# Stick-breaking attention stage: ScalarE in written order, VectorE's written order begun later, q's second copies read from SBUF, and three more products ahead of the last scores

## The chip, the cores and the metric

The kernel runs on one core of one Trainium2 chip. The metric is the device time of one execution in microseconds (us). Of the kernel before, three executions were timed and one more was run under the hardware profiler. "PE" is TensorE (matmuls; "PEld" its weight loads), "ACT" is ScalarE, "DVE" is VectorE, "POOL" is GpSimd, "SP" is the queue that issues the loads.

## The reference, cut to what matters

Two layers over 512 tokens of width 1024, in float32: layer 0 mixes tokens by stick-breaking attention (16 heads of 64), layer 1 by a gated MLP, and each is followed by a SwiGLU feed-forward part. The change lies in layer 0's attention:

```python
qkv = (h @ w_qkv).reshape(B, S, 3, SB_HEADS, SB_HEAD_DIM)
z = einsum('bhtd,bhsd->bhts', q_block, k[:, :, :kend]) * SB_HEAD_DIM ** -0.5
log_1m = where(before, log_sigmoid(-z), 0.0)
later = cumsum(log_1m, reverse=True) - log_1m
a = where(before, exp(log_sigmoid(z) + later), 0.0)
o = einsum('bhts,bhsd->bhtd', a, v[:, :, :kend])
y = o.transpose(0, 2, 1, 3).reshape(B, S, D) @ w_o
```

With s = sigmoid(-z), a weight is the difference of two neighbours in the running product of s. The kernel takes it so: tokens are laid out in reverse, a scan multiplies the sigmoids up, and a subtraction of the scan from itself, shifted by one, gives the weights.

## The kernel before, in words

**Precision.** A float32 product is done as three fast products (`mm3`): each operand is split into a high part rounded to fp32r and a low part, the rest. `split` makes the high part on ACT (L112, tiles named `wh` for weights) and the low part on DVE (`wl`).

**Weights.** All weight blocks of 512 KB stand in one list, `stream`, in the order of use. `wload` issues the next block's load on SP into one of two buffers (`raw`). `wemit` splits the next block into one of five buffer pairs (`wh`, `wl`). `wget(src, look=3)` is called where a block is used and first runs `wemit` up to three blocks further. While `dve.chain` is set, `wemit` also issues the load of the block after, ahead of the split. The condition vector's sums (`Bg`, tiles `G`, `A`, `B`, loads `rawada` in two buffers of their own) are advanced one step at a time by `bg.step`, one multiply-add on DVE per step.

**Order of work.** The framework puts each engine's instructions in an order by a plan of its own, which can move an instruction far ahead of its place in the program. Two chains overrule it: where `pe["chain"]` is set, matmuls go in written order, and the class `Written` does the same for an engine while its `chain` is set. Before the change only DVE is wrapped (`dve = Written(nc.vector)`); ACT (`act = nc.scalar`) follows the framework's plan throughout. Both chains are set at L861, just before the first pair's `evac_q`, and cleared at L912.

**The attention stage**, about 61 to 262 us of the profile, has three parts.

1. *The v phase* (L863 to L878). The products of pair 0's q and k and of the first half of v have just ended. `v_evac(0)` copies v out of four PSUM banks, `evac_q` and `evac_k` copy and split q and k, and the second half of v is computed in eight steps of 12 matmuls. Pair 0's first scores stand after step 1, its second scores after step 4.
2. *The lead-in* (L879 to L886). `fill(n)` runs n of the small products that make q and k of the later pairs (`pqk`, three matmuls each; eight make a q or a k; two PSUM banks in turn). 6 fills, pair 0's last scores, then 4, 4 and 6 fills.
3. *The pairs* (L887 to L908), eight turns. A turn transposes the weights of its pair in three groups (`flip`: LATE of 3 blocks a head, EARLY0 of 3, EARLY1 of 4; each copied from PSUM by ACT into `ar`, L834, out of one bank per head, `tw`), computes the next pair's scores in three groups (`scores`: `z` on PE, sigmoid on ACT at L807, scan into `left` and subtraction into `ga` on DVE), multiplies with v (`values`, tile `av`) and splits the result (`finish`, tile `o`). Between them stand fills, seven numbers a turn in `FILLS`, and `Bg` steps in `SUMS`. When q's and k's products have run out, in turns 6 and 7, the fills are the first 16 products of the output projection (tile `y`).

**q's evacuation** (`evac_q`, L693). Each of two heads has its own tile half with the other head's 64 partitions filled too: ACT copies the head's half out of PSUM, scaled by 0.125 (L696); DVE makes the low part `qlow` from PSUM and that copy (L698); ACT copies the same PSUM half, scaled again, into the other 64 partitions (L703). `evac_k` (L706) makes one copy on ACT (L709) and the low part on DVE.

In a turn with fills of 2, 3, 2, 3, 2, 3, 1, the fourth fill ends a q and the twelfth ends a k; the fifth and the thirteenth begin the next product and so call `wget`, which emits one split.

Of the kernel before, what the change touches and what calls it, by code (L numbers as in the profile page):

```python
# [8 lines left out]
F32 = mybir.dt.float32  # L9
F32R = mybir.dt.float32r  # L10
AF = mybir.ActivationFunctionType
# [14 lines left out]
def trunk(ctx: ExitStack, tc: tile.TileContext, A: dict, out: bass.AP):  # L26
    nc = tc.nc
# [19 lines left out]
    def slot(dt, name, a=2, b=512):  # L47
        return s4.tile([P, a, b], dt, tag="s4", name=nm(name))

    def bank(name, tag="b"):  # L50
        return psum.tile([P, 512], F32, tag=tag, bufs=6 if tag == "b" else 2, name=nm(name))

    act = nc.scalar
    pe = {"prev": None, "chain": False}

    class Written:
# [13 lines left out]

            return call

    dve = Written(nc.vector)

    def pe_op(b):

# [607 lines left out]
    with tc.tile_pool(name="att", bufs=1) as att, tc.tile_pool(name="att2", bufs=6) as att2:  # L684
# [3 lines left out]
        own = [slice(0, 64), slice(64, P)]  # L688
# [4 lines left out]
        def evac_q(i, pq):  # L693
            q = slot(F32R, "q")
            for h in range(2):
                act.activation(q[own[h], h, :], pq[own[h], :], AF.Copy, scale=0.125)  # L696
            for h in range(2):
                dve.scalar_tensor_tensor(  # L698
                    qlow[own[h], i % 2, h, :], pq[own[h], :], 0.125,
                    q[own[h], h, :].bitcast(F32), ALU.mult, ALU.subtract,  # L700
                )
            for h in range(2):
                act.activation(q[own[1 - h], h, :], pq[own[h], :], AF.Copy, scale=0.125)  # L703
            qk[i] = [q]

        def evac_k(i, pk):  # L706
# [12 lines left out]
        def filler():  # L719

            for i in range(1, NPAIR):
                for e, evac in enumerate((evac_q, evac_k)):
                    pb = bank("pqk", "p")
                    w = wget(("wqk", i, e))
                    for k in range(KD):
                        h, l = hTk(hT, k, 0, T)
                        mm3(pb[:], w[0][:, k, :], w[1][:, k, :], h, l, k == 0, k == KD - 1)
                        if k == KD - 1:
                            evac(i, pb)
                        yield  # L730
            early["w"].extend(wget(("wo", k), 0) for k in range(NEARLY))
            for tt, y in early["y"].items():
                tok = slice(tt * P, (tt + 1) * P)
                for k, w in enumerate(early["w"]):
                    for hf in range(2):
                        if k == 0:
                            y[hf] = bank("y", "p" if tt == 3 else "b")
                        c = slice(hf * 512, (hf + 1) * 512)
                        mm3(
                            y[hf][:], o8[k][:, 0, tok], o8[k][:, 1, tok],  # L740
                            w[0][:, 0, c], w[1][:, 0, c], k == 0, False,
                        )
                        yield
# [1 line left out]
        NEARLY = 4  # L745
        FIRST = (4, 4, 6)
        FILLS = ((2, 3, 2, 3, 2, 3, 1),) * 5 + (
            (2, 2, 2, 2, 2, 2, 0), (1, 2, 1, 2, 1, 1, 0), (3, 0, 2, 0, 2, 1, 0),
        )
        SUMS = ((0, 1, 0, 1, 0, 0, 0),) * 6 + ((1, 1, 1, 1, 1, 1, 0), (1, 0, 1, 0, 1, 1, 0))  # L750
        fgen = filler()
# [1 line left out]
        def fill(n, at=None):  # L753
            for j in range(n):
                next(fgen, None)
                if j == at:
                    bg.step(1)
# [100 lines left out]

        with tc.issue_after(last_sqrt[0].ins):
            table = nc.scalar.preload_act_table_set("sigmoid_and_others")  # L860
        pe["chain"] = dve.chain = True  # L861
        evac_q(0, pq0)
        evac_k(0, pk0)  # L863
        B31, B2, B0 = (3, 1), (2,), (0,)
# [15 lines left out]
        av = bank("av")  # L880
        spare = bank("spare")
        bg.bank = lambda: spare
        fill(6, 1)
        cur[0](B0)
        for n in FIRST:
# [23 lines left out]
        for _ in fgen:  # L909
            bg.step(1)  # L910
        bg.step(99)
        pe["chain"] = dve.chain = False  # L912

    wpool2 = ctx.enter_context(tc.tile_pool(name="wpool2", bufs=1))
    wpools.append((wpool2, 1))
# [356 lines left out]
```

## Time and profile before

| | us |
|---|---|
| median of 3 executions | 1166.7 (1164.49 to 1168.05) |
| profiled execution | 1164.59 |
| its span, first to last instruction | 1162.8 |
| PE busy | 1119.7 (96%) |
| DVE busy | 869.5 (75%) |
| ACT busy | 567.8 (49%) |

A row of the timeline gives an instruction's start and duration in us, engine, source line, operation, output<-inputs and shape; "x2" after it means that two instructions that follow each other were merged; in square brackets stands how long the engine was idle before and what released it. A row of the waits gives who waited for whom, the total in us, the number of times and the longest. A row of the windows gives, for a stretch of time, its length, the busy time of PE, PEld, DVE, ACT and POOL (with instruction counts), the granted PE clock as a share of full speed, the share of time in which the 16 DMA engines were busy, and GB/s. DVE instructions all carry line L65 (the wrapper's call), matmuls L89, transposes L97. In a pipelined row of matmuls the time from start to start is the pace; the duration of one is longer.

### The profile page before, as it was taken

The numbers are of one execution on the slowest core, as the hardware profiler recorded it, in microseconds if no ns is written. First come the engines' busy times: TensorE is split into PE (matmuls) and PEld (weight loads), VectorE is DVE, ScalarE is ACT, GpSimd is POOL, SyncE is SP. The second block draws the span as 40 slices with busy tenths as digits, with TensorE's granted clock in tenths as the row PEclk, the third lists the DMA queues.
The fourth block names the chain that finished last, engine by engine and source line by source line (L and its number), as shares of the span: only waits on it lengthen the run. The fifth ranks groups of instructions, "written<-read, shape, count | busy, mean of one in ns | idle before, by whom it ended". The sixth has DMA issues, their size and how long they took to land.

```text
span 1162.8 us, 17861 instructions
## 1 busy us (share of the span) xinstructions
PE 1119.7 (96%) x7136; PEld 991.6 (85%) x7136; DVE 869.5 (75%) x1131; ACT 567.8 (49%) x951; POOL 22.0 (2%) x37
## 2 busy tenths in 40 slices
PE   4989999899999999999999999999999999999997
PEld 3767777678999999998877887988999999998886
DVE  6858898967988888778676865668989898882214
ACT  6434665655655555563143633536555555581112
POOL 0200000000000000000000100001000000000000
PEclk8989999999999999999999999999999999999999
DMA  8637343524424353438887474324334444244311
GB/s 325 223 115 243 114 128 92 162 91 145 145 91 150 125 163 128 128 114 281 282 264 235 146 253 128 127 57 163 107 126 117 158 128 145 73 144 146 94 52 73
DMA packets 48775, 173.91 MB, mean 150 GB/s; under 512 B 5674, under 2 KB 6058, under 8 KB 48692
## 3 DMA queue, kind: packets, MB, share of 16 engines
q1 hardware_dynamic: 46964, 166.48, 44.5%
q0 software_dynamic: 1728, 6.29, 1.4%
q8 instruction: 56, 0.92, 0.3%
q14 instruction: 27, 0.22, 0.1%
HBM read 164.36 MB, written 8.39 MB: 149 GB/s over the span
## 4 chain that ended last, share of the span: by engine, by line
PE 68%; DVE 13%; DMA 12%; issue 4%; ACT 3%; SPq 0%; DVEq 0%; ACTq 0%
PE r L89 30%; PE y L89 20%; DMA rawada<-in_ada 6%; PE v L89 4%; PE gu L89 4%; DVE wl L65 3%; PE pqk L89 2%; DMA rawx<-in_wx 2%; PE u L89 2%; DVE left L65 2%; DVE B L65 1%; DMA raw<-in_wqk 1%; DMA raw<-in_wdown 1%; PE tw L97 1%; PE sv L89 1%
## 5 line engine op out<-in xcount | busy, mean ns | idle before, releaser
L89 PE MATMUL y<-wh,as 128*128 128x512 f32 x832 | 263.9, 395 | 0.6 <-DVE G L65 0.6
L112 ACT ACTIVATE wh<-raw 128x1024 fp32r<-128x1024 f32 x112 | 118.3, 1060 | 213.7 <-PE y L89 100.9
L65 DVE TENSOR_TENSOR wl<-raw,wh 128x1024 fp32r<-128x1024 f32 x112 | 136.3, 1221 | 108.5 <-ACT wh L112 108.0
L89 PEld LDWEIGHTS y<-wh,as 128*128 128x128 f32 x832 | 156.2, 188 | 37.5 <-DVE G L65 1.1
L89 PE MATMUL r<-Sh,wl 128*128 128x256 f32 x608 | 170.4, 280 | 0.0
L89 PE MATMUL r<-Sh,wh 128*128 128x256 f32 x608 | 170.1, 280 | 0.0
L89 PE MATMUL r<-Sl,wh 128*128 128x256 f32 x608 | 170.1, 280 | 0.0
L89 PE MATMUL y<-wl,as 128*128 128x512 f32 x416 | 164.3, 395 | 0.0
L65 DVE TENSOR_TENSOR wl<-f,wh 128x1024 fp32r<-128x1024 f32 x76 | 92.7, 1220 | 36.8 <-ACT wh L112 36.8
L112 ACT ACTIVATE wh<-f 128x1024 fp32r<-128x1024 f32 x76 | 80.7, 1062 | 76.0 <-PE r L89 66.2
L89 PEld LDWEIGHTS r<-Sh,wh 128*128 128x128 f32 x608 | 114.7, 189 | 0.0
L89 PEld LDWEIGHTS r<-Sl,wh 128*128 128x128 f32 x608 | 114.6, 188 | 0.0
L89 PEld LDWEIGHTS r<-Sh,wl 128*128 128x128 f32 x608 | 114.6, 188 | 0.0
L89 PEld LDWEIGHTS y<-wl,as 128*128 128x128 f32 x416 | 78.2, 188 | 17.9
L89 PE MATMUL r<-hTh,wh 128*128 128x256 f32 x304 | 88.8, 293 | 1.2 <-DVE gu L65 1.2
L89 PE MATMUL r<-hTl,wh 128*128 128x256 f32 x304 | 84.8, 279 | 0.0
L89 PE MATMUL r<-hTh,wl 128*128 128x256 f32 x304 | 80.1, 280 | 0.0
L89 PEld LDWEIGHTS r<-hTh,wh 128*128 128x128 f32 x304 | 57.2, 188 | 6.5 <-DVE gu L65 2.6
L89 PE MATMUL r<-hTh,b 128*128 128x256 f32 x304 | 60.7, 282 | 0.0
L89 PE MATMUL v<-wh,hTh 128*128 128x512 f32 x128 | 52.9, 413 | 5.1 <-ACT hTh L628 5.1
L89 PE MATMUL v<-wl,hTh 128*128 128x512 f32 x128 | 52.6, 411 | 5.0 <-DVE wl L65 5.0
L89 PEld LDWEIGHTS r<-hTl,wh 128*128 128x128 f32 x304 | 57.3, 188 | 0.1
(197 smaller groups left out, 2444.0 us busy)
## 6 DMA issues: line engine op xcount, KB each, us to landing
rawada<-in_ada SPq DMA_DIRECT2D x80, 512.0 KB, 4.9
raw<-in_wdown SPq DMA_DIRECT2D x44, 512.0 KB, 4.1
rawy<-in_wy SPq DMA_DIRECT2D x38, 512.0 KB, 3.6
rawx<-in_wx SPq DMA_DIRECT2D x38, 512.0 KB, 4.5
raw<-in_wqk SPq DMA_DIRECT2D x16, 512.0 KB, 4.3
ada<-in_ada0p SPq DMA_DIRECT2D x12, 512.0 KB, 8.1
raw<-in_wgu SPq DMA_DIRECT2D x12, 512.0 KB, 4.2
xd<-x POOLq DMA_DIRECT2D x12, 512.0 KB, 2.9
```

The source lines that it names most:

```text
L65: b = f(*a, **k)
L89: b = nc.tensor.matmul(o, l, r, start=start, stop=stop, skip_group_check=True)
L97: last_tp[0] = nc.tensor.transpose(o, i, ident)
L112: act.activation(hi, src, AF.Copy)
```

## The change

```diff
@@ -50,7 +50,6 @@
-    act = nc.scalar
     pe = {"prev": None, "chain": False}
@@ -70,7 +69,7 @@
-    dve = Written(nc.vector)
+    dve, act = Written(nc.vector), Written(nc.scalar)
@@ -700,7 +699,7 @@ (evac_q)
             for h in range(2):
-                act.activation(q[own[1 - h], h, :], pq[own[h], :], AF.Copy, scale=0.125)
+                act.activation(q[own[1 - h], h, :], q[own[h], h, :].bitcast(F32), AF.Copy)
             qk[i] = [q]
@@ -745,7 +744,7 @@
         FILLS = ((2, 3, 2, 3, 2, 3, 1),) * 5 + (
-            (2, 2, 2, 2, 2, 2, 0), (1, 2, 1, 2, 1, 1, 0), (3, 0, 2, 0, 2, 1, 0),
+            (2, 2, 2, 2, 2, 2, 0), (4, 2, 1, 1, 0, 0, 0), (3, 0, 2, 0, 2, 1, 0),
         )
@@ -858,7 +857,7 @@ (ahead of the v phase)
-        pe["chain"] = dve.chain = True
+        pe["chain"] = True
         evac_q(0, pq0)
@@ -880,6 +879,7 @@ (after the v phase)
         bg.bank = lambda: spare
+        dve.chain = act.chain = True
         fill(6, 1)
@@ -909,7 +909,7 @@ (after the last turn)
-        pe["chain"] = dve.chain = False
+        pe["chain"] = dve.chain = act.chain = False
```

It has four edits. ACT is wrapped as DVE is, and from the lead-in to the end of the attention stage it issues in written order. DVE's written order begins at the lead-in, so that in the v phase DVE follows the framework's plan, and `wemit`, which looks at `dve.chain`, issues no load ahead there. q's second copies read the first copy in SBUF in place of PSUM. In turn 6 the eight fills are spread as 4, 2, 1, 1, 0, 0, 0, so that four and no longer one stand ahead of the last pair's first scores.

## The prediction, made before the run

> **What bounds the kernel now.** I read the page first: PE is busy 96% of the span, so time is won only where PE stands still or runs at a low clock. Then I asked for PE's waits from 60 to 270 us, the stage that the change touches.
>
> ```profile
> PE v L89 <- DVE wl L65: 5.0, 1, 5.0
> PE tw L97 <- ACT ar L834: 4.1, 5, 1.8
> PE pqk L89 <- ACT q L703: 2.8, 1, 2.8
> PE z L89 <- DVE k L65: 2.1, 1, 2.1
> ```
>
> Four places, 14.0 us in all. The windows show what else happens at them, and how full the engines are in a turn of the pair loop.
>
> ```profile
> 64.00:70.00 6.00, 1.01 (x3) 0.82 (x3) 4.96 (x6) 3.27 (x6) 0.00 (x0) 0.83 0.00 0
> 70.00:75.00 5.00, 5.00 (x13) 3.83 (x13) 1.39 (x2) 1.68 (x2) 0.00 (x0) 0.52 0.69 213
> 95.30:113.30 18.00, 15.21 (x66) 11.95 (x65) 14.46 (x14) 9.59 (x16) 0.00 (x0) 1.00 0.66 211
> 131.10:150.27 19.17, 18.62 (x110) 14.75 (x109) 17.47 (x21) 11.70 (x22) 0.00 (x0) 1.00 0.31 90
> 226.20:244.10 17.90, 15.77 (x90) 12.26 (x88) 17.67 (x23) 9.87 (x17) 0.00 (x0) 0.90 0.47 148
> ```
>
> Two things are to be seen. In a normal turn (131.10 to 150.27) PE is the fullest engine, 18.62 of 19.17 us, with DVE close behind at 17.47 and ACT far below. And the granted clock is 0.52 right after the 5.0 us wait, and 0.90 around the 2.1 us wait; both stalls cost more than their idle time. So each of the four stalls is walked through, and for each I ask what is late next.
>
> **Part 1: VectorE's order in the v phase.** DVE and ACT around the 5.0 us wait:
>
> ```profile
> 56.58 1.05 ACT L112 ACTIVATE wh<-raw 128x1024 fp32r<-128x1024 f32 x1
> ```
> ```profile
> 64.95 1.39 DVE L65 SCALAR_TENSOR_TENSOR qlow<-pq,q 64x512 fp32r<-64x512 f32 x2 [7.55 <-ACT q L696]
> 66.38 1.39 DVE L65 TENSOR_TENSOR k<-pk,k 64x512 fp32r<-64x512 f32 x2
> 67.80 2.36 DVE L65 TENSOR_TENSOR wl<-raw,wh 128x1024 fp32r<-128x1024 f32 x2
> ```
>
> PE's second half of v waits for the first `wl` at 67.80. Its inputs were there at 56.58 + 1.05 = 57.6, and DVE stood idle for 7.55 us; only the written order, which puts q's and k's low parts first, held it. Without that order nothing holds the two `wl` back, and PE can go on at about 64. Gain 5.0. The slow clock goes with the wait: in the chain of waits 23 matmuls at half clock take 8.21 us, and 9 at full clock took 2.10, 0.233 each.
>
> ```profile
> 50.38 2.10 PE v L89 x9
> 69.08 8.21 PE v L89 x23
> ```
>
> 23 at 0.233 are 5.4, so another 2.8 us are saved. The moved order also takes the extra load ahead out of `wemit` in this phase and lets the sums `G` run early: their loads wait on SP behind the weights'. Neither is on PE's path as long as `qlow` and `k` come by PE's first scores, 24 matmuls or 5.6 us after 64; two such pairs of instructions, 2.78 us from 64.95, end at 67.8, 1.8 us early, and one sum in front of them fits. On the other side, DVE may take up a `wl` just before something of the start that PE needs: at most 2.36 / 2 = 1.2, at best nothing; I take 0.3, since the 7.55 us of idle time are the nearer row.
>
> The Trainium skill (TensorE: Matmul & The Clock Gate, section "Why this matters for your kernels") asks for no PE gap over about 3 us, since one idle window of about 3.4 us halves the clock. The 5.0 us wait and its 0.52 agree with it.
>
> **Part 2: the lead-in.** The third product group needs a PSUM bank that q of pair 1 still holds:
>
> ```profile
> 107.41 0.40 PE L89 MATMUL pqk<-hTh,wl 128*128 128x512 f32 x1
> 110.59 0.50 PE L89 MATMUL pqk<-hTh,wh 128*128 128x512 f32 x1 [2.79 <-ACT q L703]
> ```
> ```profile
> 107.92 1.39 DVE L65 SCALAR_TENSOR_TENSOR qlow<-pqk,q 64x512 fp32r<-64x512 f32 x2
> ```
> ```profile
> 109.35 1.19 ACT L703 ACTIVATE q<-pqk 64x512 fp32r<-64x512 f32 x2 [1.48 <-DVE qlow L65]
> ```
>
> The bank is read by ACT, then DVE, then ACT again. With the copies from SBUF the last reader is `qlow`, so 110.54 - 109.31 = 1.2 us go for certain. The rest hangs on `qlow`, which was late because DVE in the window 95.30 to 113.30 was idle for 3.5 of 18 us, partly behind sums whose loads had not landed:
>
> ```profile
> DVE G L65 <- DMA rawada<-in_ada: 4.5, 4, 1.4
> ```
>
> PE will come here 5.0 + 2.8 = 7.8 us earlier, at about 99.8, so `qlow` must end 109.31 - 99.8 = 9.5 us earlier than it did. DVE gets 2.36 us of `wl` and some sums out of the way before 64, and loses the 4.5 us of load waits if the sums start that early; with the 3.61 us that it idled from 70 to 75 (5.00 less 1.39) that makes 10.5. It just suffices. Bounds: gain 1.2 less nothing to 2.8; I take 2.8, and leave the other end to a rival. The copies themselves: 0.60 us each from PSUM; the nearest ACT row from SBUF, 0.63 for 512 elements on twice the partitions, makes it 0.03 more, hidden on an engine with 7 us of free time a turn.
>
> ```profile
> 236.18 0.63 ACT L112 ACTIVATE acch<-G 128x512 fp32r<-128x512 f32 x1 [0.51 <-PE spare L89]
> ```
>
> **Part 3: ScalarE in written order in the turns.** One turn, SP, ACT, PE, DVE:
>
> ```profile
> 136.30 8.74 SPq L106 DMA_DIRECT2D raw<-in_wqk  x2
> ```
> ```profile
> 139.82 1.06 ACT L112 ACTIVATE wh<-raw 128x1024 fp32r<-128x1024 f32 x1 [3.92 <-DMA raw<-in_wqk]
> 140.78 1.18 ACT L696 ACTIVATE q<-pqk 64x512 fp32r<-64x512 f32 x2
> 141.98 0.87 ACT L834 ACTIVATE ar<-tw 128x384 f32<-128x384 f32 x2
> 143.42 1.20 ACT L703 ACTIVATE q<-pqk 64x512 fp32r<-64x512 f32 x2 [0.28 <-DVE qlow L65]
> ```
> ```profile
> 136.26 0.39 PE L89 MATMUL pqk<-hTh,wl 128*128 128x512 f32 x1
> 137.19 0.82 PE L97 MATMUL tw<-identt,ga 128*128 128x128 f32 x6
> 141.58 0.40 PE L89 MATMUL pqk<-hTh,wl 128*128 128x512 f32 x1
> 142.53 1.09 PE L97 MATMUL tw<-identt,ga 128*128 128x128 f32 x8 [0.55 <-ACT ar L834]
> ```
> ```profile
> 153.93 1.22 DVE L65 TENSOR_TENSOR wl<-raw,wh 128x1024 fp32r<-128x1024 f32 x1
> ```
>
> ACT's planned order puts the `wh` of the next block first. It waits 3.92 us for a load that was issued at 136.30, and it is needed only by the `wl` at 153.93. Behind it stand q, whose products ended at 136.65, and `ar`, which frees the banks for the 8 transposes. In written order q comes first: from 136.65 two q (1.18), two copies (1.20), the `wh` of a block older, whose `wl` is the next (1.06), and two `ar` (0.87) end at 140.96. PE wants the banks at 141.58 + 0.24 = 141.82, so the wait goes with 0.86 us to spare. All five waits of this kind are 4.1. In turn 5 one product fewer (3 x 0.233 = 0.70) lies between, which leaves 0.16; I give back 0.2.
>
> The change queues things behind waits on ACT too: behind q's wait for PE now stand the copies, a split and `ar`; behind the k copies the sigmoids of the last scores. The sum above holds them. DVE gets q about 4 us earlier (140.78 less 136.65); PE, at 18.62 us a turn, is what remains.
>
> **Part 4: four products ahead of the last scores.** PE and DVE in turns 6 and 7:
>
> ```profile
> 227.41 0.40 PE L89 MATMUL y<-wh,o 128*128 128x512 f32 x1
> 229.94 0.33 PE L89 MATMUL z<-k,q 128*128 128x128 f32 x1 [2.13 <-DVE k L65]
> 247.40 0.82 PE L97 MATMUL tw<-identt,ga 128*128 128x128 f32 x6
> ```
> ```profile
> 229.20 1.41 DVE L65 TENSOR_TENSOR k<-pqk,k 64x512 fp32r<-64x512 f32 x2
> 244.26 1.23 DVE L65 TENSOR_TENSOR ga<-left 128x1024 f32<-128x1024 f32 x1
> ```
> ```profile
> 230.00:234.00 4.00, 4.00 (x16) 3.14 (x17) 3.97 (x6) 1.19 (x2) 0.00 (x0) 0.73 0.61 193
> 234.00:238.00 4.00, 4.00 (x21) 3.52 (x20) 4.00 (x6) 2.17 (x5) 0.00 (x0) 0.85 0.33 116
> ```
>
> Three more products take 2.1 us and cover the wait of 2.1. The slow clock after it is worth 4.00 x 0.27 + 4.00 x 0.15 = 1.7. But those products are taken from between these scores and the transposes at 247.40, which need the `ga` that ends at 245.49. DVE works from `k` to that `ga` without a pause (17.67 of 17.90 busy), 245.49 - 229.94 = 15.55 after the scores; PE's way there shrinks from 17.46 to 17.46 - 2.1 - 1.7 = 13.7. So PE waits there for up to 1.9 us, less what DVE is ahead; I take 1.5 back.
>
> By the same rule of the Trainium skill a wait of 2.1 us is too short to halve the clock; the 0.73 behind it disagrees.
>
> **The sum.** 5.0 + 2.8 - 0.3 + 2.8 + 4.1 - 0.2 + 2.1 + 1.7 - 1.5 = 16.5 us. Behind the stage PE hardly waits and takes the gain on. The profiled execution, 1164.59 (span 1162.8 and 1.8 around it), becomes 1148.1; it lies 2.1 below the median of 1166.7, so for the median I say **1150.2**.
>
> **The rivals.**
> - *Half of the front is given back (1155.5).* The framework's plan puts sums that wait for loads ahead of `qlow` and `k` in the v phase: one load wait of up to 1.4 and one sum of 1.3 at the first scores (2.7), and the lead-in keeps 1.6 to 2.8 of its wait. For it: the 10.5 against 9.5 of part 2. Against: PE's 1.8 us of room. 1150.2 + 2.7 + 2.6 = 1155.5.
> - *The clock dip in turn 6 has another cause (1151.9).* Then 1.7 stays. For it: after the 2.79 us wait of the lead-in the clock was 1.00. By the Trainium skill's rule above this would be the case. Against: it is the only dip in the turns, and it lies right behind the wait.
> - *No change (1166.7).* DVE becomes the bound and PE waits for it wherever it gains. For it: 17.47 busy. Against: 18.62 for PE is more, and DVE itself waits for q.
> - *Slower (1173.7).* In written order ACT meets each turn's `wh` before its load has landed, at the place behind the q copies, and waits the 3.92 of above there, with `ar` behind it: six turns x 3.92 = 23.5, so 1150.2 + 23.5. It decides once a load lands later than 139.1 (136.65 + 1.18 + 1.20) for the block whose `wl` is the next one. Against: loads land about one block earlier than that, since the one landed at 139.82 was for a `wl` at 153.93.
>
> **How the numbers follow.** Forecast 0.60, half of the front 0.20, clock 0.08, no change 0.07, slower 0.05. The range 1146 to 1157.5: downward, if nothing is given back (2.0) and pace is won beyond the idle rows, upward to the first rival and its bounds; outside lie the last two and a little of the others. About 0.3%, 3.5 us, is what a measurement of this kernel tells from no change: faster 0.88, same 0.07, slower 0.05.
>
> **What would show it.** Right: PE's wait for `wl` gone, no half clock at 69; the v phase 7.5 us shorter; no wait for ACT q L703; turns of about 18.5 us, each `wh` directly ahead of its `wl` in time and without a wait for a load; a small wait of the transposes on DVE's `ga` in turn 7. Wrong: new PE waits on `qlow` or `k` of pair 0 or 1, ACT idle on loads ahead of `ar`, or turns still of 19.1 us.

## The result, and the profile after

| | before | after |
|---|---|---|
| median (us) | 1166.96 of 4 (1164.49 to 1168.05) | 1151.72 of 4 (1148.75 to 1153.22) |
| profiled execution, its span | 1164.59, 1162.8 | 1153.22, 1151.4 |

The ratio is 0.9869 [0.9844, 0.9894]: faster by 15.2 us, where 16.5 were forecast. The two profiled executions are only 11.4 us apart in span: that of before took 2.4 less than its median, that of after 1.5 more than its own, and 11.4 + 2.4 + 1.5 = 15.3. Before the steps of the prediction are judged, the 11.4 us are laid out by stage.

PE's waits from 60 to 270 us come first, in after. The columns are who waited for whom, the total in us, the times and the longest.

```profile
PE pqk L88 <- DVE qlow L64: 2.1, 1, 2.1
PE y L88 <- DVE k L64: 2.1, 1, 2.1
```

Of 14.0 us in four places, 4.2 are left in two, and both are new. (After has one code line less: matmuls are L88, and DVE and ACT both carry L64, the line of the wrapper.) The marks between the stages are the two evacuations of v on ACT and the products with v (`av`) of pairs 0, 5 and 7 on PE. In before:

```profile
61.79 2.07 ACT L599 ACTIVATE V<-v 128x512 f32<-128x512 f32 x4 [4.16 <-PE v L89]
95.80 2.04 ACT L599 ACTIVATE V<-v 128x512 f32<-128x512 f32 x4
```
```profile
128.78 2.38 PE L89 MATMUL av<-ar,V 128*64 128x128 f32 x24
223.91 2.38 PE L89 MATMUL av<-ar,V 128*64 128x128 f32 x24
252.97 2.38 PE L89 MATMUL av<-ar,V 128*64 128x128 f32 x24
```

In after:

```profile
64.25 2.07 ACT L64 ACTIVATE V<-v 128x512 f32<-128x512 f32 x4 [3.57 <-PE v L88]
89.64 2.06 ACT L64 ACTIVATE V<-v 128x512 f32<-128x512 f32 x4 [3.96 <-PE v L88]
```
```profile
124.26 2.38 PE L88 MATMUL av<-ar,V 128*64 128x128 f32 x24
214.18 2.38 PE L88 MATMUL av<-ar,V 128*64 128x128 f32 x24
242.95 2.38 PE L88 MATMUL av<-ar,V 128*64 128x128 f32 x24
```

Differences of neighbouring marks give the table (us).

| stage | before | after | gain | forecast |
|---|---|---|---|---|
| start to first evacuation of v | 61.79 | 64.25 | -2.46 | -0.3 |
| v phase, to the second | 34.01 | 25.39 | 8.62 | 7.8 |
| lead-in, to `av` of pair 0 | 32.98 | 34.62 | -1.64 | 2.8 |
| five turns, to `av` of pair 5 | 95.13 | 89.92 | 5.21 | 3.9 |
| two turns, to `av` of pair 7 | 29.06 | 28.77 | 0.29 | 2.3 |
| the rest | 909.83 | 908.45 | 1.38 | 0 |
| span | 1162.8 | 1151.4 | 11.4 | 16.5 |

The v phase and the turns did more than was forecast, the lead-in and the last turns failed, and the start lost. How good the turns became is seen in the windows of the first and the fifth of them in after (columns as in the prediction: length, busy time of PE, PEld, DVE, ACT and POOL, granted clock, DMA share, GB/s):

```profile
124.26:142.67 18.41, 18.41 (x109) 14.84 (x109) 17.35 (x21) 11.77 (x22) 0.00 (x0) 1.00 0.37 116
197.85:214.18 16.33, 16.33 (x101) 13.15 (x100) 15.22 (x19) 9.87 (x19) 0.00 (x0) 1.00 0.35 102
```

PE is busy for the whole of each turn: 18.41 of 18.41. Nothing is left to win there by another order. ACT in the first of these turns:

```profile
132.18 1.22 ACT L64 ACTIVATE q<-pqk 64x512 fp32r<-64x512 f32 x2 [0.80 <-PE pqk L88]
133.30 1.27 ACT L64 ACTIVATE q<-q 64x512 fp32r<-64x512 f32 x2
134.59 1.06 ACT L64 ACTIVATE wh<-raw 128x1024 fp32r<-128x1024 f32 x1
135.68 0.87 ACT L64 ACTIVATE ar<-tw 128x384 f32<-128x384 f32 x2
```

q, its copies, a split and `ar` follow each other without a pause, and the split waits for no load, where it had waited 3.92 us. From 124 to 243 us ACT waits for no load at all.

The two new waits as the timeline of PE has them, in the lead-in and in turn 6, and DVE in the v phase, the lead-in and turn 6:

```profile
104.56 0.47 PE L88 MATMUL pqk<-hTh,wh 128*128 128x512 f32 x1 [2.14 <-DVE qlow L64]
...
220.15 0.47 PE L88 MATMUL y<-wh,o 128*128 128x512 f32 x1 [2.08 <-DVE k L64]
```
```profile
73.51 1.28 DVE L64 SCALAR_TENSOR_TENSOR G<-rawada,sc,G 128x1024 f32<-128x1024 f32 x1
...
89.56 1.28 DVE L64 SCALAR_TENSOR_TENSOR G<-rawada,sc,G 128x1024 f32<-128x1024 f32 x1 [1.20 <-DMA rawada<-in_ada]
93.17 1.28 DVE L64 SCALAR_TENSOR_TENSOR G<-rawada,sc,G 128x1024 f32<-128x1024 f32 x1 [2.32 <-DMA rawada<-in_ada]
95.47 1.28 DVE L64 SCALAR_TENSOR_TENSOR G<-rawada,sc,G 128x1024 f32<-128x1024 f32 x1 [1.01 <-DMA rawada<-in_ada]
...
103.03 1.39 DVE L64 SCALAR_TENSOR_TENSOR qlow<-pqk,q 64x512 fp32r<-64x512 f32 x2
...
218.61 1.39 DVE L64 TENSOR_TENSOR k<-pqk,k 64x512 fp32r<-64x512 f32 x2
```

The first sum of the stage runs at 73.51, in the v phase and not ahead of it. DVE then stands idle for 1.20 + 2.32 + 1.01 = 4.5 us in front of sums whose loads have not landed, and `qlow` of pair 1 starts at 103.03, 4.9 us earlier than before (107.92). PE comes for its bank at 104.56 - 2.14 = 102.4, 5.4 earlier than before (110.59 - 2.79). In turn 6 the second of the four products that now stand ahead of the last scores takes the other PSUM bank, and there k of pair 7 lies until DVE has read it at 220.0.

Each of these waits is followed by a stretch at half clock, and the start has one too:

```profile
42.00:62.00 20.00, 18.35 (x81) 14.66 (x80) 14.03 (x25) 8.91 (x12) 5.98 (x8) 0.91 0.43 136
100.00:112.00 12.00, 9.86 (x42) 7.75 (x41) 11.75 (x12) 3.64 (x7) 0.00 (x0) 0.86 0.67 223
216.00:228.00 12.00, 9.92 (x48) 8.05 (x45) 10.56 (x14) 5.83 (x10) 0.00 (x0) 0.86 0.72 218
```

A clock of 0.86 over 12 us is 0.14 x 12 = 1.7 us of PE work lost; 0.09 x 20 is 1.8 (1.7 by windows of 1 us, which show half clock from 47.5 to 51). Before has 1.00 in the first two of these windows; the half clock of its turn 6 lies at 231 to 235 us.

### The profile page after: what moved, and what is told of

Its sections match the earlier page's. It is cut to its first block, busy times and chain, and to the rows that moved or that the text cites. A ratio compares the mean times of both kernels' runs of the same rounds, so it can differ in the third digit from the quotient of the medians.

```text
span 1151.4 us, 17842 instructions
## 1 busy us (share of the span) xinstructions
PE 1118.6 (97%) x7136; PEld 993.1 (86%) x7136; DVE 869.3 (75%) x1131; ACT 568.5 (49%) x951; POOL 22.1 (2%) x37
## 4 chain that ended last, share of the span: by engine, by line
PE 76%; DVE 9%; DMA 9%; issue 3%; ACT 2%; SPq 0%; DVEq 0%; ACTq 0%
PE r L88 32%; PE y L88 20%; PE pqk L88 6%; DMA rawada<-in_ada 5%; PE gu L88 4%; PE v L88 4%; PE u L88 2%; DVE wl L64 2%; PE z L88 2%; PE tw L96 1%; PE av L88 1%; DVE G L64 1%; DMA raw<-in_wdown 1%; PE tp L96 1%; PE sv L88 1%
## 5 line engine op out<-in xcount | busy, mean ns | idle before, releaser
L88 PE MATMUL y<-wh,as 128*128 128x512 f32 x832 | 264.0, 395 | 0.5 <-DVE G L64 0.5
L64 DVE TENSOR_TENSOR wl<-raw,wh 128x1024 fp32r<-128x1024 f32 x112 | 136.3, 1222 | 107.0 <-ACT wh L64 106.7
L64 ACT ACTIVATE wh<-raw 128x1024 fp32r<-128x1024 f32 x112 | 118.2, 1060 | 179.2 <-PE y L88 99.0
L88 PEld LDWEIGHTS y<-wh,as 128*128 128x128 f32 x832 | 156.2, 188 | 37.6 <-DVE G L64 1.0
L88 PE MATMUL r<-Sh,wl 128*128 128x256 f32 x608 | 170.4, 280 | 0.0
L88 PE MATMUL r<-Sh,wh 128*128 128x256 f32 x608 | 170.1, 280 | 0.0
L88 PE MATMUL r<-Sl,wh 128*128 128x256 f32 x608 | 170.1, 280 | 0.0
L88 PE MATMUL y<-wl,as 128*128 128x512 f32 x416 | 164.3, 395 | 0.0
L64 DVE TENSOR_TENSOR wl<-f,wh 128x1024 fp32r<-128x1024 f32 x76 | 92.8, 1222 | 36.7 <-ACT wh L64 36.7
L64 ACT ACTIVATE wh<-f 128x1024 fp32r<-128x1024 f32 x76 | 80.7, 1061 | 74.7 <-PE r L88 64.9
L88 PEld LDWEIGHTS r<-Sh,wh 128*128 128x128 f32 x608 | 114.7, 189 | 0.0
L88 PEld LDWEIGHTS r<-Sl,wh 128*128 128x128 f32 x608 | 114.6, 188 | 0.0
L88 PEld LDWEIGHTS r<-Sh,wl 128*128 128x128 f32 x608 | 114.6, 188 | 0.0
L88 PEld LDWEIGHTS y<-wl,as 128*128 128x128 f32 x416 | 78.2, 188 | 17.9
L88 PE MATMUL r<-hTh,wh 128*128 128x256 f32 x304 | 88.8, 293 | 0.0
L88 PE MATMUL r<-hTl,wh 128*128 128x256 f32 x304 | 84.8, 279 | 0.0
L88 PE MATMUL r<-hTh,wl 128*128 128x256 f32 x304 | 80.1, 280 | 0.0
L64 ACT ACTIVATE e<-r 128x256 f32<-128x256 f32 x114 | 43.5, 381 | 53.0 <-PE r L88 52.8
L88 PEld LDWEIGHTS r<-hTh,wh 128*128 128x128 f32 x304 | 57.2, 188 | 5.2 <-DVE gu L64 1.2
L88 PE MATMUL r<-hTh,b 128*128 128x256 f32 x304 | 60.6, 282 | 0.0
L88 PE MATMUL v<-wh,hTh 128*128 128x512 f32 x128 | 52.1, 407 | 6.1 <-ACT hTh L64 6.1
L88 PEld LDWEIGHTS r<-hTl,wh 128*128 128x128 f32 x304 | 57.3, 188 | 0.1
```

Of the source, the lines that this page charges most:

```text
L64: b = f(*a, **k)
L88: b = nc.tensor.matmul(o, l, r, start=start, stop=stop, skip_group_check=True)
```

## The experiments

There were twelve runs, in three groups, each beside runs of before on its own chip (medians of before there 1166.05, 1165.17 and 1164.98). Ratios are to before.

### One half of the change at a time

**VectorE's order alone.** Before, with only this:

```diff
-        pe["chain"] = dve.chain = True
+        pe["chain"] = True
         evac_q(0, pq0)
...
+        dve.chain = True
         fill(6, 1)
```

> The kernel before with one edit: VectorE's written order begins at the lead-in, as in the change; ScalarE, the copies and the products are as before. Theory (the parts add up): the v phase is 8.6 us shorter as in the changed kernel, PE no longer waits for the first wl, the five waits of the transposes on ar (4.1 us) and the wait on k (2.1) stay, and the start loses up to 1.3 us because one wl is planned between two sums that PE waits for: about 1160 us. Rival (ScalarE's order is what shortens the stage, and the early wl only moves the wait to pair 0's first scores): 1165 to 1168 us, with a new PE wait of some 5 us in the v phase.

Measured: 1158.57 us (1158.16 to 1160.62), ratio 0.9941 [0.9926, 0.9957]. Its waits from 60 to 270 us and the window behind the first of them:

```profile
PE pqk L89 <- ACT q L703: 4.1, 1, 4.1
PE tw L97 <- ACT ar L834: 3.6, 4, 1.8
PE z L89 <- DVE k L65: 2.1, 1, 2.1
```
```profile
99.00:111.00 12.00, 7.91 (x29) 6.05 (x28) 11.18 (x12) 4.79 (x8) 0.00 (x0) 0.72 0.67 216
```

The wait for `wl` is gone, and the v phase is as short as in after (evacuations at 61.85 and 87.24), so the rival fell. In after DVE makes the second half's low parts well ahead of `qlow` (67.42): one in the start, at 51.50 (its row stands further down), and one at

```profile
60.71 1.23 DVE L64 TENSOR_TENSOR wl<-raw,wh 128x1024 fp32r<-128x1024 f32 x1 [0.25 <-ACT wh L64]
```

Part of that gain is given back at once in the lead-in, whose wait grows from 2.8 to 4.1. The window's 12 x 0.28 = 3.4 us of lost clock set in at 101.9, 2.2 us before this wait ends, so that about 2.3 of them fall on PE's work.

**ScalarE's order and q's copies alone.** After, with VectorE's order and the fills as before:

```diff
-            (2, 2, 2, 2, 2, 2, 0), (4, 2, 1, 1, 0, 0, 0), (3, 0, 2, 0, 2, 1, 0),
+            (2, 2, 2, 2, 2, 2, 0), (1, 2, 1, 2, 1, 1, 0), (3, 0, 2, 0, 2, 1, 0),
...
-        pe["chain"] = True
+        pe["chain"] = dve.chain = True
...
-        dve.chain = act.chain = True
+        act.chain = True
```

> ScalarE in written order from the lead-in on and the copies from SBUF; VectorE's written order and the products as before. Theory (the parts add up): the wait of 5.0 us for the first wl and the slow clock behind it stay, the waits on ar go, turns 1 to 5 take 18.4 us in place of 19.1 to 19.4 (5.2 us in all), the lead-in gains 1.2 us: about 1160.5 us. Rival (the turns gain only because VectorE comes to them earlier): the turns stay above 19 us and the time is 1165 to 1168 us.

Measured: 1158.98 us (1156.4 to 1160.64), ratio 0.9939 [0.9922, 0.9955].

```profile
PE v L88 <- DVE wl L64: 6.0, 1, 6.0
PE pqk L88 <- DVE qlow L64: 1.5, 1, 1.5
PE z L88 <- DVE k L64: 1.3, 1, 1.3
```

(One wait of 0.2 is left off.) No `ar` is waited for any more, the turns are 18.4 us, and the wait for `wl` stays, all as expected. The two halves give 7.5 and 7.1 us, together 14.6 of the 15.2.

This kernel also separates the loss in the start. Its VectorE order there is that of before, yet its first evacuation of v comes at 63.76, 2.0 later than before, and its start has this window:

```profile
30.00:42.00 12.00, 10.99 (x45) 8.76 (x44) 11.64 (x19) 5.05 (x7) 0.53 (x1) 0.86 0.85 319
```

The clock is 1.00 there in before. So 1.7 us come with a half-clock window that VectorE's order did not bring. Nine of the twelve profiles of this section have such a window between 35 and 40 us; before and after do not, and what sets it these runs don't show.

**q's copies from PSUM again**, all else as in after:

```diff
-                act.activation(q[own[1 - h], h, :], q[own[h], h, :].bitcast(F32), AF.Copy)
+                act.activation(q[own[1 - h], h, :], pq[own[h], :], AF.Copy, scale=0.125)
```

> The changed kernel, but q's second copies read PSUM again. Theory (in written order the copies would stop ScalarE, since they share the bank with VectorE's qlow and must wait for it): copies start about 2.7 us later in each turn, ar and with it the four-block transposes come late by about 1.5 us a turn, turns take 19 to 20 us, and the lead-in's bank is freed 1.2 us later: about 1160 us, with PE waits on ar. Rival (the copies are off the path with 7 us of free time on ScalarE a turn, as the prediction had it): 1151 to 1153 us.

Measured: 1162.11 us (1159.69 to 1164.68), ratio 0.9969 [0.9956, 0.9982]. It is only 3.9 us under the before of its chip, so about 11 of the 15 us are lost, and the rival fell. ACT in one turn, and PE's waits:

```profile
135.52 1.20 ACT L64 ACTIVATE q<-pqk 64x512 fp32r<-64x512 f32 x2 [0.80 <-PE pqk L88]
139.23 1.20 ACT L64 ACTIVATE q<-pqk 64x512 fp32r<-64x512 f32 x2 [2.51 <-DVE qlow L64]
140.32 1.04 ACT L64 ACTIVATE wh<-raw 128x1024 fp32r<-128x1024 f32 x1
141.39 0.87 ACT L64 ACTIVATE ar<-tw 128x384 f32<-128x384 f32 x2
```
```profile
PE tw L96 <- ACT ar L64: 7.4, 6, 1.6
PE pqk L88 <- ACT q L64: 3.3, 1, 3.3
```

(A third, of 2.2 for `y`, is left off.) In written order the second copies come directly behind the first. From PSUM they wait 2.51 us for DVE, which reads the same bank for `qlow`, and a split and `ar` stand behind them. Turns are 19.74 us (`av` at 127.62 and 147.36), longer than the 19.17 of before; in the turns ScalarE's order pays only together with the copies from SBUF. The copies from SBUF without ScalarE's order were not run, so what they give alone is not shown. The Trainium skill (PSUM — Partial Sum Buffer, section "PSUM bank collisions raise a hardware error") says that the compiler makes two engines' accesses to one bank and quadrant wait for each other, reads too; the 2.51 us behind `qlow` agree.

**Turn 6's fills as before**, all else as in after: `(4, 2, 1, 1, 0, 0, 0)` back to `(1, 2, 1, 2, 1, 1, 0)`.

> The changed kernel with the products of turn 6 spread as before (1, 2, 1, 2, 1, 1, 0). Theory (the four products ahead of the last scores gained nothing: the second of them needs the PSUM bank that k of pair 7 holds, and so waits for the same VectorE instruction as the scores did): PE waits about 2 us for k at the scores instead, and the time is within 1 us of the changed kernel, 1151 to 1152 us. Rival (part 4 of the prediction): 2.3 us slower, 1154 us.

Measured: 1153.88 us (1146.8 to 1155.88), ratio 0.9884 [0.9859, 0.991]: no difference from after that could be measured. The median is the rival's 1154, but the last turns did not become slower: from `av` of pair 5 to that of pair 7 it takes 27.36 us (216.69 to 244.05) with no half clock, where after takes 28.77 with one. What is longer in this profile is the wait in the lead-in, 3.8 us, though the program there is that of after. The old wait, of `z` for k, is not the 2 us that was expected but only 1.3, as it was with ScalarE's order alone, where these two turns take 27.36 too (220.21 to 247.57). So ScalarE's order with the copies has already taken 1.7 of the 29.06 of before, and the edit swaps the 1.3 that remain for the 2.08 at the bank and a half clock.

### Taking the two new waits away

**The output projection's products by halves**, so that the second bank is wanted only by the fifth product:

```diff
-                for k, w in enumerate(early["w"]):
-                    for hf in range(2):
+                for hf in range(2):
+                    for k, w in enumerate(early["w"]):
```

> The changed kernel, but the first products of the output projection run through all four weight blocks for one half of the columns and then for the other, so that the four products ahead of the last scores all go to the bank that q of pair 7 left long ago. Theory (the second product waits for the bank that k of pair 7 holds until VectorE has read it): the wait of PE for k, 2.1 us, goes and so may the half clock behind it; VectorE is then the bound up to the transposes of turn 7, so that 1 to 2 us remain of it: 1149.5 to 1150.5 us, with a new wait on ga. Rival (it isn't the bank: whatever stands there waits for k): the wait of 2 us stays at the second product or at the scores and the time is that of the changed kernel, 1151 to 1153 us.

Measured: 1151.37 us (1148.04 to 1154.1), ratio 0.9887 [0.986, 0.9914]. The wait stays, as the rival had it, for something else:

```profile
220.20 0.79 PE L88 MATMUL y<-wl,o 128*128 128x512 f32 x1 [2.21 <-DVE wl L64]
```

The fourth product of a half takes the fourth block of weights, whose low part stands behind k on DVE.

**Pair 0's last scores behind the first group of the lead-in**, so that PE has other work ahead of the wait for `qlow`:

```diff
+        fill(FIRST[0], 1)
...
-        for n in FIRST:
+        for n in FIRST[1:]:
```

> The changed kernel with pair 0's last scores four products later, behind the first group of the lead-in's 4, 4 and 6, so that VectorE makes qlow of pair 1 ahead of the scans of these scores. Theory (the wait of the lead-in is VectorE's queue: 3.6 us of scan and subtraction stand in front of qlow): the wait on qlow, 2.1 to 3.8 us in two profiles, and the half clock behind it go: 1146 to 1149 us. Rival (the sums that wait for their loads set the time at which VectorE gets there, and the scans only fill it): the wait shrinks by less than 1 us and the time is 1151 to 1153 us.

Measured: 1151.51 us (1150.89 to 1153.69), ratio 0.9891 [0.9868, 0.9915].

```profile
109.17 0.33 PE L88 MATMUL z<-k,q 128*128 128x128 f32 x1 [1.97 <-DVE k L64]
```

The wait for `qlow` is gone, but the 1146 to 1149 us that were expected did not come: 4.6 us later a wait nearly as long is there, for the next thing on DVE.

**Both together.**

> The edits of the two runs before together. Theory (two separate waits): the gains add up, 1145 to 1147.5 us, and no PE wait over 1 us is left between 65 and 215 us. Rival (VectorE is the bound by then, and what is won at the lead-in is waited for in turn 7): no better than the better of the two by more than 0.5 us.

Measured: 1152.4 us (1148.47 to 1154.99), ratio 0.9897 [0.9868, 0.9926], where 1145 to 1147.5 were expected; waits of 2.2 (`y` on `wl`) and 1.1 (`z` on k). In this profile the lead-in is 2.3 us shorter than in after (32.28), without half clock behind the 1.1, but with the same lead-in program the run before had 1.97 there and gained nothing. Changing what PE asks for first takes no wait away reliably where DVE itself is late.

**DVE relieved.** The three sums of v steps 5 to 7 go into turns 0 to 2:

```diff
-        SUMS = ((0, 1, 0, 1, 0, 0, 0),) * 6 + (...)
+        SUMS = ((0, 1, 0, 1, 0, 1, 0),) * 3 + ((0, 1, 0, 1, 0, 0, 0),) * 3 + (...)
...
-            bg.step(1)
+            bg.step(int(k < 5))
```

> The changed kernel with three of the twelve sums of the v phase and the lead-in moved into the turns 0 to 2, one each; the scores stay where they are. It separates the two halves of the lead-in's wait. If the sums and their loads hold VectorE up (the rival of the run with the scores later): the wait on qlow goes, and the three turns get longer by up to 0.4 us each, as VectorE then has 18.7 us of work in 18.4: 1147 to 1150 us. If only the scans ahead of qlow hold it up: a wait of 1 us or more stays, 1150 to 1153 us.

Measured: 1149.94 us (1148.39 to 1152.23), ratio 0.9878 [0.9854, 0.9902].

```profile
99.36 1.39 DVE L64 SCALAR_TENSOR_TENSOR qlow<-pqk,q 64x512 fp32r<-64x512 f32 x2
```

The time is the expected one. `qlow` starts 3.7 us earlier than in after. The wait in the lead-in is gone, the lead-in takes 30.7 us (second evacuation of v at 89.75, `av` at 120.45) in place of 34.62, which is 2.14 and a 1.7 of half clock and 0.1, and the turns stay at 18.4. What made DVE late were the sums and their loads. The loads set the length: five profiles (after, turn 6's fills as before, products by halves, and the free bank and the control below) have the same program in the lead-in, and there DVE waits 4.84, 6.60, 4.97, 4.35 and 4.99 us for loads ahead of `qlow`, and PE then waits 2.14, 3.79, 2.27, 1.72 and 2.31: each time the loads' time less 2.6 to 2.8. The three profiles with the sums moved have no such load wait and no PE wait. The median is not told apart from that of after, since the wait in turn 6 stays and the two were timed on different chips; the next group has a control.

### Both causes together, beside a control

**The bank and the fourth block.** The first eight products go (k, half) = (0,0), (1,0), (2,0), (0,1), (1,1), (2,1), (3,0), (3,1), and turn 6's fills become 3, 2, 2, 1, 0, 0, 0.

> The changed kernel with one edit: in the first token tile the output projection's first eight products go (k, half) = (0,0), (1,0), (2,0), (0,1), (1,1), (2,1), (3,0), (3,1), so that the second bank is wanted only by the fourth product and the fourth block's low part only by the seventh; turn 6's fills become 3, 2, 2, 1, 0, 0, 0. Theory: the 2.1 us wait of turn 6 came from two things in a row, the bank of k of pair 7 and behind it the low part of the fourth block; with neither wanted early there is no wait for either, the time from av(5) to av(7) is about 27 us where the changed kernel had 28.8, and the median is 1 to 2 us under that of the control on this chip. Rival: the DVE queue itself is late there and whatever is next on it is waited for: a wait of 1 to 2 us for k, ga or wl stays in turn 6 or 7, and the median is that of the control within 1 us.

**That and the moved sums.**

> The order of products and fills of e11_free_bank, and also the condition vector's three sums of v steps 5 to 7 moved into turns 0 to 2 (one more in each), which took the lead-in's wait away when done alone. Theory: the lead-in and turn 6 have separate causes, so both waits go: from the second v_evac to the first av about 30.7 us, turns still 18.4, no wait over 1 us on PE from 64 to 240 us, and a median 2 to 4 us under the control, about 1147 to 1149. Rival: DVE, with a sum more in three turns, becomes the bound there: the turns get longer than 18.4 by up to 0.9 us each and the median does not go under that of the control by more than 1 us.

**That and the start**, where the low parts that may slip in are ordered behind the last `hTl`:

```diff
+        if hold and n < 8:
+            order(dve.prev, hold[0])
...
+        if b == 3:
+            hold.append(dve.prev)
```

> e12_bank_and_sums, and also the first splits on DVE of the weight blocks for v ordered behind the last low part of hT at the start, which the change had freed to go in between. Theory: the start lost 2.5 us in the profile, about 0.6 of it from such a hoisted low part and the rest from a half-clock window that falls where it will; so the first V evacuation comes about 0.6 us earlier than in e12_bank_and_sums (compared without a half-clock window), and the median is 0.6 us lower, within the intervals. Rival: the low parts then come late for the second half of v and a wait of 1 to 5 us for wl returns; the median is 1 to 5 us higher than that of e12_bank_and_sums.

**The changed kernel again.**

> The changed kernel once more, the same program, to have it on the same chip as the three others. Theory: 1150.5 to 1152.5, the two waits of 2.1 us in the lead-in and in turn 6 as before. Rival: if the half-clock windows are set by the program and not by chance, their places (two in the start, one in the lead-in, one in turn 6) are the same as in the first profile of this kernel; if they run free, some of them are absent or elsewhere.

| kernel | median (us) | ratio to before |
|---|---|---|
| free bank | 1150.16 (1147.95 to 1153.88) | 0.9879 [0.9856, 0.9903] |
| free bank and sums | 1144.25 (1142.77 to 1149.51) | 0.9829 [0.9801, 0.9858] |
| and the start | 1145.95 (1142.39 to 1147.3) | 0.9833 [0.9808, 0.9859] |
| control | 1153.2 (1150.27 to 1155.97) | 0.9901 [0.9879, 0.9922] |

The free bank alone is 3.0 us under the control, where 1 to 2 were expected, with intervals that overlap. In its profile the last turns take 26.8, as expected; its lead-in, which this edit does not touch, happened to be 2.1 shorter. With the sums it is 9.0 under it, and the intervals do not touch: this version beats both before and the changed kernel, by more than the 2 to 4 us expected. The two profiles are only 4.5 apart (1145.72 and 1150.27); in them the lead-in gives 4.1 and the last turns 2.0, the start 1.7, and the part behind the attention stage takes 3.2 back. So 6.1 us are shown to come from the two waits; the rest of the 9.0 is not accounted for. All that PE waits for between 60 and 270 us in this version is the following (`spare` is the PSUM bank of the condition vector's sums):

```profile
PE spare L88 <- DVE G L64: 1.0, 1, 1.0
```

No 2 us wait is left, and no half clock in the stage. From `av` of pair 5 to that of pair 7 it takes 26.8 us (209.23 to 236.05), 2.2 less than before but only 0.5 less than with the old fills. DVE is now the fullest engine there:

```profile
209.23:226.00 16.77, 15.69 (x103) 11.90 (x104) 16.50 (x22) 11.26 (x21) 0.00 (x0) 1.00 0.59 180
```

The edit at the start shows in its profile and not in its time. The low part no longer lies between the last two sums of the start (`acc` x2 in one row), and from PE's last long wait there to the first evacuation (at 61.04) it is 15.88 us, as in before (45.93 to 61.79, 15.86):

```profile
45.16 0.50 PE L88 MATMUL v<-wh,hTh 128*128 128x512 f32 x1 [1.34 <-ACT hTh L64]
```
```profile
49.72 1.53 DVE L64 SCALAR_TENSOR_TENSOR acc<-ada,sc,acc 128x512 f32<-128x512 f32 x2
```
```profile
46.27 0.50 PE L88 MATMUL v<-wh,hTh 128*128 128x512 f32 x1 [1.35 <-ACT hTh L64]
```
```profile
50.83 0.75 DVE L64 SCALAR_TENSOR_TENSOR acc<-ada,sc,acc 128x512 f32<-128x512 f32 x1
51.50 1.22 DVE L64 TENSOR_TENSOR wl<-raw,wh 128x1024 fp32r<-128x1024 f32 x1
52.63 0.75 DVE L64 SCALAR_TENSOR_TENSOR acc<-ada,sc,acc 128x512 f32<-128x512 f32 x1
```

The lower two views are of after: 64.25 - 46.27 = 17.98 with a `wl` between the sums. In nine profiles with that `wl` and no half clock in this stretch it takes 16.43 to 16.47 us, so the low part that slipped in costs about 0.6, as expected, and the other 1.5 of after go with its half-clock window. The median is 1.7 above that of the version without this edit, as the rival had it, but no wait for `wl` came back; within such ranges it says nothing either way.

The control, expected at 1150.5 to 1152.5, took a little more. It has the waits of after, 2.3 in the lead-in and 2.1 in turn 6, each followed by half clock again. (The row of the first names ACT's `wh` as its end; `qlow` ended 0.15 us before PE went on, as it did in after with 0.14.) In the start, besides the half clock around 20 us that all profiles have, it has windows from 28 and from 48 us; the first profile of this program has only the one from 48. So the windows in the stage follow the waits, and of those in the start one came again and one did not.

## Why the prediction was right, and where its steps were not

**Right in the time and the sign, in part by luck:** 1151.7 against 1150.2, inside the range. In the two profiles the terms add up to 11.4 and not to 16.5: the lead-in, the last turns and the start fell 8.6 short, and the v phase, the turns and the rest gave 3.5 more. That the medians are 15.2 apart all the same is because the profiled execution of before, from which the sum was made, was a quick one and that of after a slow one.

**Part 1, the v phase: right.** 8.6 against 7.8. The wait and the slow clock behind it went together. The "0.3" for a `wl` taken up too early was right in kind; it costs 0.6. Of the 2.46 lost in the start, another 1.5 are the half-clock window at 48 us, and 0.34 are there already at PE's first product of v (20.79 against 20.45), which was not followed up.

**Part 2, the lead-in: wrong by 4.4 us.** The step that failed is that the sums would run early and lose their 4.5 us of load waits. The first sum ran at 73.51, after the 64 us by which "some sums" were to be out of the way, and the waits are 4.5 us still. Of the 9.5 us by which `qlow` had to come earlier it came 4.9 earlier, and 2.1 us of wait with 1.7 of half clock were the price. The first rival had this loss in it, as 1.6 to 2.8 of the wait that stay, without the half clock; its other half, a wait at the first scores, did not come. The experiment with the moved sums shows the cause: without them DVE is in time.

**The copies from SBUF: under-priced.** Part 2 counted 1.2 us for them, in the lead-in. Part 3 put "two q, two copies" in a row on ACT without saying that this holds only for copies that don't wait for `qlow`. Taking them out of the changed kernel loses about 11 us, since ScalarE's order without them lengthens the turns.

**Part 3, the turns: right, and better.** The waits for `ar` went. 5.2 against 3.9: a wait costs PE more than the idle time named in its row. In before a turn had 18.62 us of busy PE, in after 18.41 for the same work; 0.2 a turn is most of the 1.3 between. The kernel with VectorE's order alone shows the same within one profile: 18.46 in its first turn, which has no wait, and 18.62 and 18.61 in the next two, with waits of 0.35 and 0.40. What PE loses there, no run shows.

**Part 4, the last turns: wrong by 2.0 us.** The step that failed is that three more products would cover the wait. They need the second PSUM bank, and k of the last pair lies in it until DVE has read it: the cover waited for the very instruction it should have covered. That could have been read in the code (two banks in turn) and was not asked. The wait was also no longer the 2.1 of the sum: ScalarE's order with the copies had cut it to 1.3, and with the old fills these turns take 27.36, 1.7 less than before. The edit cost 1.4 of that again. With the products reordered and the sums moved 2.2 came, near the forecast 2.3, but by another way: 1.7 of it without this edit and 0.5 by the new order. DVE is full there, as forecast, only that PE's wait for it (1.0) shows at `spare` and none at the transposes behind `ga`.

**Rivals.** "No change" and "slower" fell: PE is busy 18.41 of 18.41 in a turn, and each `wh` found its load landed. That the clock dip has another cause fell too, though its 1151.9 lies nearest to what was measured, which is chance: in the stage, half clock stands in no profile anywhere but behind a wait, and where the wait of turn 6 is 1.3 or less there is none.

The 1.4 us that the rest of the kernel gained are not shown to come from the change: between the two profiles of the changed kernel (after and the control) that part differs by 3.8 us (908.45 and 904.61).

## What to carry to other kernels

Before work is moved to cover a wait, ask which buffer it writes and which operands it reads: if either hangs on the engine that is late, the wait only changes its name, as it did here in the change itself, with the products by halves and with the scores later. An order written by hand for an engine pays when no instruction early in it waits for a third engine; look for reads that can come from SBUF in place of a shared PSUM bank first. Where two waits are short, remove the cause (work queued ahead on the late engine) and not the one that shows.

## What the runs showed of the hardware

The price of a short PE wait has a step. Over the profiles of before, after and the experiments, from 60 to 270 us: waits of PE up to 1.8 us were never followed by a lower clock. Of fourteen between 1.97 and 2.8 us, eleven were followed by half clock, ten times for a stretch that costs 1.7 us more, one time (products by halves) for twice that; three were not (2.79 in before, 2.15 with copies from PSUM, 2.27 with products by halves). All five of 3.3 us and over (5.0, 4.1, 6.0, 3.3, 3.8) were followed by half clock for about 6.8 us, which set in 1.1 to 2.2 us before the wait ended and cost 2.3 to 2.9 us of PE work behind it. An estimate from these rows: a wait of 2 us costs 2 to 4 us, once 5.5, and one cut from 2.14 to 1.72, as it fell out in the lead-in of the kernel with the free bank, can save another 1.7. Whether 1.8 and 1.97 are the true edges, these runs don't show. The Trainium skill (TensorE: Matmul & The Clock Gate, section "Why this matters for your kernels") warns of gaps over about 3 us; the 2.08 and 2.14 us waits here, with 0.86 behind them, say that 2 us are enough at times.
